# A decoder layer on one core: the convolutions read PSUM, four banks held throughout, and the last two chunks' down rows in one sum

## The chip, the cores and the metric

The kernel runs on one core of one Trainium2 chip. The core has five engines, each with its own queue of instructions, worked off in order: TensorE (PE in the profile, with its weight loads as PEld) does the matmuls and writes only to PSUM; VectorE (DVE) and ScalarE (ACT) do elementwise work and read and write both SBUF and PSUM; GpSimd (POOL) does elementwise work on SBUF; SyncE (SP) issues most DMAs. PSUM has eight banks of 128 partitions x 512 float32. The metric is the device time of one execution in microseconds (us).

## The reference

One decoder layer for 1024 tokens of width 1024, all in float32. The first half of the layer is a token mixer: two groups of heads (chunked gated linear attention, and sliding-window attention with sinks), an output projection and a residual. The change is almost wholly in the second half, the gated MLP:

```
x = x + concat([o_gla, o_swa]) @ w_out
h2 = rms_norm(x, ffn_norm)
u = causal_dwconv(h2 @ w_up, conv_w, conv_b)        # 3 taps along the tokens, per channel, plus a bias
a, b = split(u, 2)                                   # 2816 channels each
out = x + (silu(a) * b) @ w_down
```

The convolution takes, for each channel and token t, `u[t]*w2 + u[t-1]*w1 + u[t-2]*w0 + bias`, with zeros ahead of the first token.

## The kernel before

**Numbers.** Each float32 operand of a large matmul is split into a high part and a low part (`split`, L82: ACT casts the high part, VectorE or GpSimd subtracts it to get the low part), and a product is three passes of matmuls, high x high, high x low, low x high (`PASSES`). A matmul here has 128 x 128 weights and 512 columns.

**Chunks.** The 2816 channels are 22 chunks of 128. For chunk `ch` the up projection gives an a side (`ua`, to be gated by SiLU) and a b side (`ub`), each 128 channels x 1024 tokens, that is two halves of 512 tokens per side. The two sides and the two token halves together are a 2 x 2 block product with the inner dimension cut in two, and chunks 1 to 20 compute it with seven products instead of eight (a Strassen-Winograd form): `SEQ` = P1, P2, P6, P5, P7, P3, P4, each of 12 matmuls. P6, P7 and P4 are added onto the bank of P1, P3 onto the bank of P5 (`ONTO`, L734), so a chunk has three banks. What a bank holds after each product is one of the four results, or a part of it:

- after P1, copied to SBUF by ACT (`ca`, first half); P2 + that copy = a side, first half
- after P6, copied to SBUF (`ca`, second half); after P5, copied to SBUF (`p5`); P7's bank + `p5` = b side, second half
- P3's bank + `ca`, second half = a side, second half
- after P4, the bank of P1 itself is the b side, first half

Chunks 0 and 21 (`PLAIN`) use the eight ordinary products in four banks: P1, R1, P2, R2, X1 to X4.

**After each product** `post` (L782) does the elementwise work: VectorE adds the copy to the bank, with the sum in SBUF (`ca`, `p5`); ACT forms `u = y*w2 + bias` and VectorE adds two taps (`conv` L759, `tap` L756), each one `scalar_tensor_tensor` over 512 tokens (511 or 510 where it starts a half). Where a half continues the one before it, `conv_edge` (L767) adds the first two columns from the last two columns of the half before. ACT takes SiLU of the a side, and VectorE multiplies a and b (`glu`, L778). The sums of the a side lie side by side in `ca`, so its second half needs no edge.

**The down projection** also runs in pairs of chunks, with seven products of two units each (`down_pair`, L894): a unit is six matmuls into a pair of banks, then one VectorE add of 1024 columns onto the accumulator `acc` in SBUF (L908). The operand sums of a pair are made on VectorE (`down_g`, L881: L885 to L889) and GpSimd (`down_w`). `dg` and `dw` are the split operands. The ten pairs are chunks 0 to 19. Chunks 20 and 21 go row by row: `down_row(ch, t)` (L925) does one chunk's contribution to 128 tokens, six matmuls into a pair of banks, then one add of 1024 columns for chunk 20, or two adds of 512 and two stores to DRAM for chunk 21. Five rows of chunk 20 are placed among the products of chunk 21 (`LAST_ROWS`).

**Banks.** `bank()` takes tiles by turns from one pool of eight banks. Just ahead of chunk 2 `open_banks` (L610) closes this pool and opens two others in its place: `psu`, four single banks taken by turns for P1, P2 and P5, and `psd`, two pairs for the down projection. A tile waits until what its memory held before has been read.

**The order.** A list of events with due times (`at`, `at_us`) sets the order in which the code issues work: one product (`MM` = 2.8) and one unit (`UNIT` = 1.4) by turns from chunk 2 on, two units per product near the end. A scheduler with a model of the engines' times may still exchange instructions on an engine's queue.

## Time and profile before

| | |
|---|---|
| median of 3 runs | 1130.04 us (1128.08 to 1131.04) |
| the profiled execution | 1130.23 us |
| its span, first to last instruction | 1128.5 us |
| TensorE matmuls | 1080.7 us busy (96%), 5156 |
| VectorE | 865.9 us (77%), 1251 |
| GpSimd | 689.9 us (61%), 518 |
| ScalarE | 478.0 us (42%), 946 |
| HBM traffic | 55 GB/s over the span |

The busy share in 40 equal slices of 28.2 us, in tenths (9 is 90% or more), with the granted TensorE clock in tenths of full speed:

```profile
PE   7999999999999999699999999999999999999897
DVE  6647456766231588668989999999989898999967
POOL 5456323334450456767878798887878787978420
PEclk9999999999999999899999999999999999999999
```

The mixer and the output projection fill the first 15 slices. The seventeenth, where TensorE falls to 0.6, holds chunks 0 and 1 of the MLP; then VectorE is at 0.8 or above until the end. A row of the timeline reads: start in us, duration, engine, line, instruction, output <- inputs, shapes, count, and in brackets the idle time ahead of it with what ended it. Matmuls are pipelined: one shows about 0.4 us, though the next starts sooner.

### The profile page before, as it was taken

The numbers are of one execution on the slowest core, as the hardware profiler recorded it, in microseconds if no ns is written. First come the engines' busy times: TensorE is split into PE (matmuls) and PEld (weight loads), VectorE is DVE, ScalarE is ACT, GpSimd is POOL, SyncE is SP. The second block draws the span as 40 slices with busy tenths as digits, with TensorE's granted clock in tenths as the row PEclk, the third lists the DMA queues.
The fourth block names the chain that finished last, engine by engine and source line by source line (L and its number), as shares of the span: only waits on it lengthen the run. The fifth ranks groups of instructions, "written<-read, shape, count | busy, mean of one in ns | idle before, by whom it ended". The sixth has DMA issues, their size and how long they took to land.

```text
span 1128.5 us, 14126 instructions
## 1 busy us (share of the span) xinstructions
PE 1080.7 (96%) x5156; PEld 860.6 (76%) x5156; DVE 865.9 (77%) x1251; ACT 478.0 (42%) x946; POOL 689.9 (61%) x518
## 2 busy tenths in 40 slices
PE   7999999999999999699999999999999999999897
PEld 5897777777888878588787777878787878777684
DVE  6647456766231588668989999999989898999967
ACT  5326664434230354434444444344443444443430
POOL 5456323334450456767878798887878787978420
PEclk9999999999999999899999999999999999999999
DMA  6124123002034201112111111112121211111103
GB/s 209 46 77 122 41 57 75 20 1 76 1 108 153 57 1 56 56 38 75 38 56 37 50 45 57 56 47 66 38 75 38 75 37 46 36 51 55 57 1 149
DMA packets 67344, 67.16 MB, mean 60 GB/s; under 512 B 4616, under 2 KB 51913, under 8 KB 67274
## 3 DMA queue, kind: packets, MB, share of 16 engines
q1 hardware_dynamic: 63432, 61.53, 17.4%
q10 hardware_dynamic: 3842, 4.73, 1.8%
q8 instruction: 41, 0.67, 0.3%
q14 instruction: 29, 0.24, 0.1%
HBM read 57.33 MB, written 4.19 MB: 55 GB/s over the span
## 4 chain that ended last, share of the span: by engine, by line
PE 67%; DVE 27%; issue 2%; ACT 2%; DMA 1%; POOL 0%; SPq 0%; ACTq 0%; POOLq 0%
PE P L749 20%; PE dn_P L904 11%; PE do L286 5%; DVE ub L757 4%; DVE ua L757 4%; PE dg L286 4%; PE dr L286 4%; DVE acc L908 4%; PE dv L286 4%; PE dq L286 3%; DVE ub L780 3%; DVE dg L87 2%; PE X L749 2%; PE dk L286 2%; DVE ub L887 1%
## 5 line engine op out<-in xcount | busy, mean ns | idle before, releaser
L904 PE MATMUL dn_P<-dw,dg 128*128 128x512 f32 x840 | 217.8, 394 | 21.3 <-DVE acc L908 14.4
L904 PEld LDWEIGHTS dn_P<-dw,dg 128*128 128x128 f32 x840 | 155.7, 188 | 65.3 <-DVE acc L908 19.9
L908 DVE TENSOR_TENSOR acc<-acc,dn_P 128x1024 f32<-128x1024 f32 x140 | 169.5, 1211 | 41.2 <-PE dn_P L904 41.0
L757 DVE SCALAR_TENSOR_TENSOR ua<-ca,cc,ua 128x511 f32<-128x511 f32 (+1 forms) x80 | 95.9, 1199 | 2.7 <-ACT ua L762 1.8
L87 POOL TENSOR_TENSOR dw<-dn,dw 128x512 fp32r<-128x512 f32 x50 | 82.9, 1658 | 19.4 <-ACT dw L84 19.4
L286 PE MATMUL do<-wow,big 128*128 128x512 f32 x384 | 91.6, 397 | 0.0
L286 PEld LDWEIGHTS do<-wow,big 128*128 128x128 f32 x384 | 71.5, 188 | 16.9 <-ACT wow L84 0.2
L749 PE MATMUL P<-big,A11w 128*128 128x512 f32 x264 | 68.0, 406 | 10.4 <-DVE ub L757 9.5
L424 POOL TENSOR_TENSOR pr<-pr,sm 128x1024 f32<-128x1024 f32 (+1 forms) x16 | 28.6, 1788 | 66.9 <-DVE sm L422 51.2
L749 PEld LDWEIGHTS P<-big,A11w 128*128 128x128 f32 x264 | 50.8, 194 | 23.7 <-issue 9.9
L749 PE MATMUL P<-big,A12w 128*128 128x512 f32 x264 | 65.5, 396 | 0.0
L780 DVE TENSOR_TENSOR ub<-ua,ub 128x512 f32<-128x512 f32 (+1 forms) x45 | 63.1, 1402 | 0.8
L757 DVE SCALAR_TENSOR_TENSOR ub<-p,cc,ub 128x511 f32<-128x511 f32 (+1 forms) x40 | 57.2, 1431 | 4.5 <-ACT ub L762 4.1
L749 PE MATMUL P<-ex,S3w 128*128 128x512 f32 x240 | 59.6, 397 | 0.2 <-ACT ca L793 0.2
L749 PE MATMUL P<-big,S1w 128*128 128x512 f32 x240 | 59.7, 396 | 0.0
L749 PE MATMUL P<-ex,S2w 128*128 128x512 f32 x240 | 59.7, 396 | 0.0
L749 PE MATMUL P<-ex,A22w 128*128 128x512 f32 x240 | 59.7, 396 | 0.0
L749 PE MATMUL P<-big,S4w 128*128 128x512 f32 x240 | 59.6, 396 | 0.0
L762 ACT ACTIVATE ua<-ca,cc 128x512 f32<-128x512 f32 x40 | 32.7, 818 | 62.9 <-DVE ca L804 44.2
L749 PEld LDWEIGHTS P<-big,A12w 128*128 128x128 f32 x264 | 49.6, 188 | 11.8 <-ACT early L821 0.2
L87 DVE TENSOR_TENSOR dg<-ub,dg 128x512 fp32r<-128x512 f32 x40 | 54.3, 1357 | 2.4 <-ACT dg L84 0.5
L749 PEld LDWEIGHTS P<-ex,S3w 128*128 128x128 f32 x240 | 45.0, 188 | 11.4 <-ACT ca L793 0.6
(424 smaller groups left out, 2499.5 us busy)
## 6 DMA issues: line engine op xcount, KB each, us to landing
up<-in_w_up_dram SPq DMA_DIRECT2D x44, 512.0 KB, 3.8
dn<-in_w_down_dram SPq DMA_DIRECT2D x22, 512.0 KB, 3.5
acc<-in_x_dram SPq DMA_DIRECT2D x8, 512.0 KB, 7.7
out_dram<-acc SPq DMA_DIRECT2D x16, 256.0 KB, 2.1
xt<-in_x_dram SPq DMA_DIRECT2D x7, 512.0 KB, 4.3
qraw<-in_w_in_dram SPq DMA_DIRECT2D x4, 512.0 KB, 8.1
vraw<-in_w_in_dram SPq DMA_DIRECT2D x4, 512.0 KB, 3.5
qt<-qt ACTq DMA_DIRECT2D x16, 128.0 KB, 2.3
```

Source lines behind the costliest of these rows:

```text
L87: (eng or pool).tensor_sub(lo, src, hi.bitcast(F32))
L286: pe.matmul(pb[:, :n], lhsT=big[:, t, k, ra, :], rhs=ws[k][:, rb, :n], start=(k == 0 and i == 0), stop=(k == KD - 1 and i == 2))
L424: pool.tensor_tensor(pr[:, :, s0:], pr[:, :, s0:], den[:, hs].rearrange("p (j o) -> p j o", o=1).broadcast_to((P, 4, n)), ALU.mult)
L749: pe.matmul(pb[:, ts.start * P:ts.stop * P], lhsT=w[:, ra, k, :], rhs=b_operand(bn, k, rb)[:, ts], start=(onto is None and i == 0), stop=( ...
L757: dve.scalar_tensor_tensor(dst, src, w, dst, op0=ALU.mult, op1=ALU.add)
L762: act.activation(u[:, a:z], y[:, a:z], AF.Identity, bias=b, scale=w2)
L780: dve.tensor_mul(ub, psb["ua", ch][:, hf * 512 + a:hf * 512 + z], ub)
L887: dve.tensor_sub(a21, a11, a21)
L904: pe.matmul(pb[:, i], lhsT=g[:, ra, c:c + P], rhs=w[:, rb, :], start=(onto is None and n == 0), stop=(n == 2), skip_group_check=onto is no ...
L908: dve.tensor_add(acc, acc, pb)
```

## The change

- `bank()` takes tiles by turns from two pools of four banks, `psa` and `psb`. `open_banks` now runs ahead of chunk 1 instead of chunk 2. It closes only `psb`, puts the two pairs of the down projection there, and takes the four banks of `psa` as fixed tiles `fb0` to `fb3` that stay until the end.
- From chunk 1 on, P1, P2 and P5 of a chunk go to three of these in rotation (`up_bank`), so that the next chunk's P1 gets this chunk's P2 bank, its P2 this chunk's P5 bank, and its P5 this chunk's P1 bank. The fourth holds the b side's second half.
- The sums stay in PSUM: the adds of P2 and P3 write back into the bank, the add of P7 writes into the fourth bank, and the taps read them there. For the b side the last tap writes its sum back into the bank (`conv_in_bank`), and the gate product reads that bank (`glu_from_bank`); its first two columns, which come from the edge, are multiplied apart.
- The a side's halves now lie in two banks, so its second half needs an edge: ACT copies the last two columns of the first half to a small tile `e`, and two taps of one and two columns add them.
- P5's copy goes to `ca`; the tile `p5` is gone.
- `down_row` is replaced by `last_row(t)`: for each half of the columns, six matmuls of chunk 20 and chunk 21 are summed in one bank, then one add of 512 columns and one store. Rows 0, 1, 4, 5 use the pairs, rows 2, 3, 6, 7 the fixed banks. All eight rows come after the last product.

```diff
     ps_first = ExitStack()
-    ps = {"b": ps_first.enter_context(tc.tile_pool(name="ps", bufs=8, space=PSUM))}
+    ps = {"a": ctx.enter_context(tc.tile_pool(name="psa", bufs=4, space=PSUM)),
+          "b": ps_first.enter_context(tc.tile_pool(name="psb", bufs=4, space=PSUM)), "n": 0}
 
     def bank(name):
-        return ps["b"].tile([P, 512], F32, tag="b", name=name)
+        ps["n"] += 1
+        return ps["ab"[ps["n"] % 2]].tile([P, 512], F32, tag="b", name=name)
...
     def open_banks():
         ps_first.close()
-        ps["b"] = ctx.enter_context(tc.tile_pool(name="psu", bufs=4, space=PSUM))
         ps["d"] = ctx.enter_context(tc.tile_pool(name="psd", bufs=2, space=PSUM))
+        ps["f"] = [ps["a"].tile([P, 512], F32, tag="b", name=f"fb{i}") for i in range(4)]
...
+    ORDER = {"P1": 0, "P2": 1, "P5": 2}
+    ORDER_PLAIN = {"P1": 0, "R1": 1, "X1": 2, "X3": 3}
+
+    def up_bank(ch, name):
+        i = (ORDER_PLAIN if ch in PLAIN else ORDER)[name]
+        return ps["f"][3 if i == 3 else (ch - 1 + i) % 3]
...
+    def conv_in_bank(ch, u, y):
+
+        ci = NCH + ch
+        w0, w1, w2, b = (cc[:, i, ci:ci + 1] for i in range(4))
+        act.activation(u, y, AF.Identity, bias=b, scale=w2)
+        tap(u[:, 1:512], y[:, 0:511], w1)
+        dve.scalar_tensor_tensor(y[:, 0:510], y[:, 0:510], w0, u[:, 2:512], op0=ALU.mult, op1=ALU.add)
+
+    def glu_from_bank(ch, hf, y):
+        u = psb["c", ch, hf]
+        ua = psb["ua", ch][:, hf * 512:hf * 512 + 512]
+        dve.tensor_mul(u[:, 2:512], ua[:, 2:512], y[:, 0:510])
+        dve.tensor_mul(u[:, 0:2], ua[:, 0:2], u[:, 0:2])
...
         elif name == "P2":
-            ca = psb["ca", ch]
-            dve.tensor_add(ca[:, 0:512], ca[:, 0:512], pb)
+            dve.tensor_add(pb, psb["ca", ch][:, 0:512], pb)
             ua = psb["ua", ch] = wide_tile(f"ua{ch}", "ua")
-            conv(ch, 0, ua, ca, 0, 512, True)
+            conv(ch, 0, ua, pb, 0, 512, True)
+            e = psb["e", ch] = fin["ff"].tile([P, 2], F32, tag="e", name=f"e{ch}", bufs=2)
+            act.copy(e, pb[:, 510:512])
...
         elif name == "P5":
-            p5 = psb["p5", ch] = half_tile(f"p5_{ch}")
-            act.copy(p5, pb)
+            act.copy(psb["ca", ch][:, 0:512], pb)
         elif name == "P7":
-            p5 = psb["p5", ch]
-            dve.tensor_add(p5, p5, pb)
+            v = psb["v", ch] = ps["f"][3]
+            dve.tensor_add(v, psb["ca", ch][:, 0:512], pb)
             ub = psb["c", ch, 1] = half_tile(f"ub1_{ch}")
-            conv(ch, 1, ub, p5, 0, 512, True)
+            conv_in_bank(ch, ub, v)
         elif name == "P3":
-            ca, ua = psb["ca", ch], psb["ua", ch]
-            dve.tensor_add(ca[:, 512:], ca[:, 512:], pb)
-            conv(ch, 0, ua, ca, 512, 1024, False)
+            ua = psb["ua", ch]
+            dve.tensor_add(pb, psb["ca", ch][:, 512:], pb)
+            conv(ch, 0, ua[:, 512:], pb, 0, 512, True)
+            conv_edge(ch, 0, ua[:, 512:], psb["e", ch])
             silu(ua)
         elif name == "P4":
             ub = psb["c", ch, 0] = half_tile(f"ub0_{ch}")
-            conv(ch, 1, ub, pb, 0, 512, True)
+            conv_in_bank(ch, ub, pb)
             conv_edge(ch, 1, psb["c", ch, 1], pb[:, 510:512])
-            glu(ch, 0)
-            glu(ch, 1)
+            glu_from_bank(ch, 0, pb)
+            glu_from_bank(ch, 1, psb["v", ch])
...
+    def last_row(t):
+        if t % 4 < 2:
+            pair = two_banks(f"dl{t}")
+            pbs = [pair[:, 0], pair[:, 1]]
+        else:
+            pbs = [ps["f"][i] for i in ((2, 0), (1, 3))[t % 4 - 2]]
+        for hf, pb in enumerate(pbs):
+            for ch in (NCH - 2, NCH - 1):
+                g, w = gtiles[ch, t // 4], blocks["d", ch, hf]
+                for i, (ra, rb) in enumerate(PASSES[::-1]):
+                    pe.matmul(pb, lhsT=g[:, ra, (t % 4) * P:(t % 4 + 1) * P], rhs=w[:, rb, :],
+                              start=(ch == NCH - 2 and i == 0), stop=(ch == NCH - 1 and i == 2))
+            acc, cs = fin["all"][:, t], slice(hf * 512, hf * 512 + 512)
+            dve.tensor_add(acc[:, cs], acc[:, cs], pb)
+            sp.dma_start(out[t * P:(t + 1) * P, cs], acc[:, cs])
...
-    at_us(starts[2, 0] - 0.05, open_banks)
+    at_us(starts[1, 0] - 0.05, open_banks)
```

What this does to the queues is shown at three places. First TensorE, from P3 of chunk 1 to P6 of chunk 2 (A11w, A12w and so on are the split weights of the products: A11w is P1's, A12w P2's, S2w P6's, S1w P5's, S3w P7's, S4w P3's, A22w P4's; P_1 and P_2 are tiles of chunks 1 and 2). Before:

```order
L749 MATMUL P_1_4451<-big,S4w_4465 128x512 x12
L749 MATMUL P_1_4390<-ex,A22w_4484 128x512 x12
L749 MATMUL P_2_4552<-big,A11w_4514 128x512 x12
L749 MATMUL P_2_4589<-big,A12w_4534 128x512 x12
L904 MATMUL dn_P_0_4610<-dw_0_4491,dg_0_4494 128x512 x6
L904 MATMUL dn_P_1_4634<-dw_0_4491,dg_0_4494 128x512 x4
L749 MATMUL P_2_4552<-ex,S2w_4569 128x512 x12
```

And now (the fixed banks are fb):

```order
L759 MATMUL fb_4399<-big,S4w_4475 128x512 x12
L759 MATMUL fb_4398<-big,A11w_4523 128x512 x11
L759 MATMUL fb_4397<-ex,A22w_4493 128x512 x12
L759 MATMUL fb_4398<-big,A11w_4523 128x512
L929 MATMUL dn_P_0_4616<-dw_0_4500,dg_0_4503 128x512 x6
L929 MATMUL dn_P_1_4640<-dw_0_4500,dg_0_4503 128x512 x6
L759 MATMUL fb_4399<-big,A12w_4545 128x512 x12
L759 MATMUL fb_4398<-ex,S2w_4574 128x512 x12
```

P1 of chunk 2 has moved ahead of P4 of chunk 1, since it no longer shares a pool with it, and the first unit of the down projection ahead of P2.

Second VectorE, from the end of chunk 9 to the sums for the fifth pair of the down projection (ub is the b side, ua the a side, D the pair's sums). Before:

```order
L757 SCALAR_TENSOR_TENSOR ub_9_6332<-P_9_6122,cc,ub_9_6332 128x510
L757 SCALAR_TENSOR_TENSOR ub_9_6271<-P_9_6122,cc,ub_9_6271 128x1
L780 TENSOR_TENSOR ub_9_6332<-ua_6174,ub_9_6332 128x512
L757 SCALAR_TENSOR_TENSOR ub_9_6271<-P_9_6122,cc,ub_9_6271 128x2
L780 TENSOR_TENSOR ub_9_6271<-ua_6174,ub_9_6271 128x512
L885 TENSOR_TENSOR D_4_6401<-ub_8_6047,ub_9_6271 128x512
L908 TENSOR_TENSOR acc<-acc,dn_P_1_6370 128x2x512
L886 TENSOR_TENSOR D_4_6402<-D_4_6401,ub_8_6107 128x512
```

And now:

```order
L798 SCALAR_TENSOR_TENSOR fb_4399<-fb_4399,cc,ub_9_6352 128x510
L804 TENSOR_TENSOR ub_9_6352<-ua_6192,ub_9_6352 128x2
L803 TENSOR_TENSOR ub_9_6289<-ua_6192,fb_4400 128x510
L767 SCALAR_TENSOR_TENSOR ub_9_6289<-fb_4399,cc,ub_9_6289 128x1
L767 SCALAR_TENSOR_TENSOR ub_9_6289<-fb_4399,cc,ub_9_6289 128x2
L803 TENSOR_TENSOR ub_9_6352<-ua_6192,fb_4399 128x510
L804 TENSOR_TENSOR ub_9_6289<-ua_6192,ub_9_6289 128x2
L933 TENSOR_TENSOR acc<-acc,dn_P_1_6391 128x2x512
L910 TENSOR_TENSOR D_4_6421<-ub_8_6063,ub_9_6289 128x512
L911 TENSOR_TENSOR D_4_6422<-D_4_6421,ub_8_6125 128x512
```

Each gate product has become one with an operand in a bank and one of two columns, and the unit's add stands ahead of the pair's sums instead of between them.

Third TensorE behind the last product (dn_0, dl_9121 and so on are banks of the rows, dnw_0 and dnw_1 the two halves of the down weights, g the gated product; of two tiles of one name the higher number is chunk 21's). Before, from X4 on:

```order
L749 MATMUL X_21_9079<-big,A22w_8948 128x512 x12
L933 MATMUL dn_2_9016<-dnw_0_8911,g_0_8914 128x512 x3
L933 MATMUL dn_2_9016<-dnw_1_8951,g_0_8914 128x512 x3
L933 MATMUL dn_3_9024<-dnw_0_8911,g_0_8914 128x512 x3
L933 MATMUL dn_3_9024<-dnw_1_8951,g_0_8914 128x512 x3
L933 MATMUL dn_4_9032<-dnw_0_8911,g_1_8954 128x512 x3
```

And now:

```order
L759 MATMUL fb_4400<-big,A22w_8990 128x512 x12
L960 MATMUL dl_9121<-dnw_0_8954,g_0_8957 128x512 x3
L960 MATMUL dl_9138<-dnw_0_8954,g_0_8957 128x512 x3
L960 MATMUL fb_4399<-dnw_0_8954,g_0_8957 128x512
L960 MATMUL dl_9121<-dnw_0_9013,g_0_9069 128x512 x3
L960 MATMUL dl_9138<-dnw_0_9013,g_0_9069 128x512 x3
L960 MATMUL fb_4399<-dnw_0_8954,g_0_8957 128x512 x2
L960 MATMUL fb_4399<-dnw_0_9013,g_0_9069 128x512 x3
```

Before, six rows of chunk 20 and then eight of chunk 21 follow X4, each with its own banks; now each bank takes three matmuls of chunk 20 and three of chunk 21, over the pairs and the fixed banks.

More of the change, by code (lines that the diff above doesn't have):

```diff
@@ L741, in product @@
         if onto is None and not part:
-            psb[name, ch] = bank(f"{name}_{ch}")
+            psb[name, ch] = up_bank(ch, name) if ch else bank(f"{name}_{ch}")
         pb = psb[name, ch] = psb[onto or name, ch]
@@ L923, in g_split @@
         split(ub[:, a:z], g[:, 0, a:z], g[:, 1, a:z], dve)
-    def down_row(ch, t):
-        pb = two_banks(f"dn{ch}_{t}")
-        g = gtiles[ch, t // 4]
-        acc = fin["all"][:, t]
-        last = ch == NCH - 1
-        for hf in range(2):
-            w = blocks["d", ch, hf]
-            for i, (ra, rb) in enumerate(PASSES[::-1] if last else PASSES):
-                pe.matmul(pb[:, hf], lhsT=g[:, ra, (t % 4) * P:(t % 4 + 1) * P], rhs=w[:, rb, :],
-                          start=(i == 0), stop=(i == 2))
-            if last:
-                cs = slice(hf * 512, hf * 512 + 512)
-                dve.tensor_add(acc[:, cs], acc[:, cs], pb[:, hf])
-                sp.dma_start(out[t * P:(t + 1) * P, cs], acc[:, cs])
-        if not last:
-            dve.tensor_add(acc, acc, pb.rearrange("p h n -> p (h n)"))
+    def last_row(t):
[13 more added lines that the diff above has]
+            sp.dma_start(out[t * P:(t + 1) * P, cs], acc[:, cs])
     ev = []
@@ L1046, in hymba_layer_kernel @@
     units = [(p, k, j) for p in range(NPAIR) for k in range(7) for j in range(2)]
-    rows = [(NCH - 2, t) for t in range(NT)]
-    LAST_ROWS = {2: 2, 3: 3}
     prods, starts, unit_at, tu = [], {}, {}, 0.0
@@ L1071, in hymba_layer_kernel @@
                     tu += UNIT
-            if ch == NCH - 1:
-                for _ in range(LAST_ROWS.get(i, 0)):
-                    at_us(tu, down_row, *rows.pop(0))
-                    tu += UNIT
     for i, name in enumerate(("P1", "R1", "P2", "R2")):
@@ L1124, in hymba_layer_kernel @@
     at_us(starts[L, 5] + MM - 0.2, lambda: g_open(L, 1, U_SLOT[L, "A12"]))
-    for ch, t in rows + [(L, t) for t in range(NT)]:
-        at_us(tu, down_row, ch, t)
-        tu += UNIT
+    for t in range(NT):
+        at_us(tu, last_row, t)
+        tu += MM
     for _, _, f, a in sorted(ev, key=lambda e: e[:2]):
```

## The prediction

> **What bounds the kernel now.** I read first the table of busy time by stage (columns: stretch, its length, busy time and instructions of PE, PEld, DVE, ACT, POOL, then granted clock, DMA share, GB/s). I cut it at the first product of chunk 3, the first product of chunk 21, the end of the last product, and the last matmul.
>
> ```profile
> 509.05:1064.72 555.67, 534.39 (x2276) 425.40 (x2274) 518.32 (x499) 242.38 (x398) 448.62 (x295) 1.00 0.17 52
> 1064.72:1099.55 34.83, 34.83 (x152) 28.18 (x151) 25.68 (x31) 13.79 (x24) 10.28 (x8) 1.00 0.05 16
> 1099.55:1124.60 25.05, 22.91 (x85) 14.10 (x83) 21.17 (x34) 1.91 (x4) 0.00 (x0) 1.00 0.36 137
> ```
>
> Chunks 3 to 20 take half the span. TensorE is busy 96% of it, but VectorE is nearly full too: 518.3 of 555.7 us, or 28.8 us for each of the 18 chunks. What TensorE takes when nothing holds it up is in two rows of the timeline (start, duration, instruction):
>
> ```profile
> 709.80 2.98 PE L749 MATMUL P<-ex,S3w 128*128 128x512 f32 x12
> 714.00 2.98 PE L749 MATMUL P<-big,S4w 128*128 128x512 f32 x12
> ```
>
> Between them lie one product and one unit of the down projection, 18 matmuls in 4.20 us, 0.233 us each. The 2274 weight loads of the stage stand for as many matmuls: 2274 x 0.233 = 530 us. So **about 25.7 us of that stage are waits of TensorE**. The table of waits says for whom (total, times, longest):
>
> ```profile
> PE dn_P L904 <- DVE acc L908: 14.4, 10, 2.0
> PE P L749 <- DVE ub L757: 9.5, 1, 9.5
> PE dn_P L904 <- ACT dw L84: 5.7, 8, 0.8
> PE dn L933 <- DVE acc L940: 1.4, 4, 0.6
> ```
>
> Rows one and three return once per pair of chunks; they are 20.1 us plus some 0.2 us of pipeline refill each. One instance:
>
> ```profile
> 737.34 1.21 DVE L908 TENSOR_TENSOR acc<-acc,dn_P 128x1024 f32<-128x1024 f32 x1
> 738.47 1.61 DVE L889 TENSOR_TENSOR D<-ub,D 128x512 f32<-128x512 f32 x1
> 740.00 3.47 DVE L757 SCALAR_TENSOR_TENSOR ua<-ca,cc,ua 128x511 f32<-128x511 f32 x2
> 743.39 1.21 DVE L908 TENSOR_TENSOR acc<-acc,dn_P 128x1024 f32<-128x1024 f32 x1
> 744.65 1.64 PE L904 MATMUL dn_P<-dw,dg 128*128 128x512 f32 x6 [1.53 <-DVE acc L908]
> ```
>
> The unit needs its pair of banks emptied by the add at 743.39, and that add stands behind two convolution taps that took 3.47 us. VectorE falls behind where the pair's extra sums (L885 to L889) are made, and TensorE waits there. So the bound is TensorE with a VectorE that is late in bursts. Two single places come on top: one wait of 9.5 us before chunk 2, and the rows at the end.
>
> **The change, part by part. 1: the convolutions on VectorE.** Groups of instructions, 520 to 1050 us (last columns: count, busy, mean ns, idle before):
>
> ```profile
> L780 DVE TENSOR_TENSOR ub<-ua,ub 128x512 f32<-128x512 f32 x34 | 51.1, 1504 | 0.6
> L757 DVE SCALAR_TENSOR_TENSOR ua<-ca,cc,ua 128x512 f32<-128x512 f32 x34 | 35.1, 1032 | 0.3
> L757 DVE SCALAR_TENSOR_TENSOR ub<-p,cc,ub 128x510 f32<-128x510 f32 x17 | 29.5, 1734 | 0.3
> L757 DVE SCALAR_TENSOR_TENSOR ua<-ca,cc,ua 128x511 f32<-128x511 f32 x17 | 25.6, 1505 | 0.0
> L757 DVE SCALAR_TENSOR_TENSOR ua<-ca,cc,ua 128x510 f32<-128x510 f32 x18 | 24.0, 1334 | 0.3
> L757 DVE SCALAR_TENSOR_TENSOR ub<-p,cc,ub 128x511 f32<-128x511 f32 x17 | 21.1, 1238 | 0.0
> L757 DVE SCALAR_TENSOR_TENSOR ub<-P,cc,ub 128x511 f32<-128x511 f32 x17 | 12.6, 741 | 0.0
> L757 DVE SCALAR_TENSOR_TENSOR ub<-P,cc,ub 128x510 f32<-128x510 f32 x17 | 12.6, 740 | 0.0
> L799 DVE TENSOR_TENSOR p<-p,P 128x512 f32<-128x512 f32 x17 | 11.5, 676 | 0.9 <-PE P L749 0.9
> L757 DVE SCALAR_TENSOR_TENSOR ub<-P,cc,ub 128x2 f32<-128x2 f32 x17 | 3.5, 208 | 0.0
> ```
>
> The same tap takes 740 ns with P (PSUM) as its source and 1030 to 1730 ns with ca or p (SBUF). Before, per chunk: three adds 3 x 0.676, taps of P2 1.505 + 1.334, of P7 1.238 + 1.734, of P3 2 x 1.032, of P4 0.741 + 0.740, two edge taps 0.42, two gate products 2 x 1.504: 14.8 us. After, all eight full taps read PSUM, 8 x 0.74, the adds stay, the gate products read one operand from PSUM (I take the add's 0.676), two edge taps 0.42: 5.92 + 2.03 + 1.35 + 0.42 = 9.72 us. New are four tiny operations with both tensors in SBUF: the two edge taps of P3 (from e) and the two-column gate products. Such operations stand only in the plain chunks now:
>
> ```profile
> 450.71 1.73 POOL L87 TENSOR_TENSOR S2w<-up,S2w 128x512 fp32r<-128x512 f32 x1
> 451.22 1.24 DVE L757 SCALAR_TENSOR_TENSOR ua<-e,cc,ua 128x1 f32<-128x1 f32 x1
> 454.29 0.21 DVE L757 SCALAR_TENSOR_TENSOR ua<-e,cc,ua 128x2 f32<-128x2 f32 x1
> 454.42 0.74 DVE L757 SCALAR_TENSOR_TENSOR ub<-early,cc,ub 128x511 f32<-128x511 f32 x1
> ```
>
> One column took 1.24 us while POOL was in an instruction, two columns 0.21 us while POOL was idle (the last row is a full tap from SBUF with POOL idle: 0.74, as from PSUM). Bounds for the four: 0.84 to 5.0 us. POOL is busy 81% of the stage, with instructions of about 1.5 us, so the mean wait is some 0.81 x 0.75 = 0.6 us and the four cost 3.3 us. Post-processing then goes from 14.8 to 13.0 us per chunk (10.6 to 14.7), VectorE from 28.8 to 27.0 us, against TensorE's 29.4. By the mean of the idle and the busy row alone it would be 2.9 us for the four, nearly the same. The Trainium skill, SBUF — State Buffer, "Who interferes with whom", says that a VectorE instruction with two SBUF inputs waits out a whole GpSimd instruction that reads SBUF, whatever its size; taken with POOL always busy that is the 5.0 us end, post-processing at 14.7 and no relief, and the 0.21 row is why I don't take it.
>
> No row shows VectorE writing PSUM, and five full operations per chunk now do, four of them in the bank they read. Bounds: as SBUF writes (0 us), or reading and writing one bank by turns, twice as long (four times 0.7, 2.8 us per chunk); below nothing isn't excluded, but no row has such an operation under 0.67. I take 0, as reading PSUM costs nothing visible beside SBUF (0.74 in both).
>
> More than the mean matters the burst. In the instance above the two taps shrink from 3.47 to 1.48, and the two gate products and taps ahead of the pair's sums lose another 2 us or so; the wait is 1.5 to 2 us. So it should close in most pairs. Late next is ACT: the new copy of e waits until VectorE's taps have read the bank, and behind it in ACT's queue stand the casts of dw and dg and the copy of P5, for which P3 waits. The second tap, at 743.5 in the instance, would end some 4 us sooner, near 739.5, the copy of P5 three or four ACT instructions later, near 742; P3 is due near 744.5 (the unit above without its wait, 743.1, and its 1.4): some 2 us of slack. I leave a fifth of the waits: **20.5 of 25.7 us gained** (bounds 0 and 25.7).
>
> **2: the entry into chunk 2.** Now the pools change there, and the first product waits until the old eight banks are all read:
>
> ```profile
> 466.61 2.96 PE L749 MATMUL P<-ex,A22w 128*128 128x512 f32 x12
> 479.10 3.32 PE L749 MATMUL P<-big,A11w 128*128 128x512 f32 x7 [9.53 <-DVE ub L757]
> 470.00:479.00 9.00, 0.00 (x0) 0.00 (x0) 8.01 (x10) 3.04 (x4) 9.00 (x7) 0.68 0.00 0
> 479.10:483.90 4.80, 4.80 (x12) 3.81 (x13) 4.59 (x5) 0.62 (x1) 2.47 (x2) 0.55 0.00 0
> 465.18 1.30 POOL L87 TENSOR_TENSOR A11w<-up,A11w 128x512 fp32r<-128x512 f32 x1
> 469.09 1.71 POOL L87 TENSOR_TENSOR A12w<-up,A12w 128x512 fp32r<-128x512 f32 x1
> 478.23 1.72 POOL L87 TENSOR_TENSOR dw<-T,dw 128x512 fp32r<-128x512 f32 x1
> 485.37 1.28 POOL L87 TENSOR_TENSOR S1w<-S,S1w 128x512 fp32r<-128x512 f32 x1 [3.71 <-ACT S1w L84]
> 499.27 1.55 PE L904 MATMUL dn_P<-dw,dg 128*128 128x512 f32 x6
> ```
>
> After, the pools change ahead of chunk 1, and P1 of chunk 2 goes to a bank that is free. A11w is ready at 466.5, so P1 runs from about 466.6, P4 of chunk 1 until 472, both halves of unit 0 until 474.8, P2 (A12w ready at 470.8) until 477.6, P6 until 480.4. What is late next is POOL: S1w comes after dw at 479.95, so at about 481.7, which holds P5 by 0.8 us; S3w comes three POOL instructions of 1.3 to 1.75 us later, at 486.5, which holds P7 by about 2 us more. P7 and unit 1 end near 491.8; before, that point is 499.27 + 1.4 = 500.7. **Gain 9 us** (bounds 0, if another wait takes its place, and 11.5, the 9.5 and 2.0 of slow clock). The 2.0 is in it: the 12 matmuls after the gap took 4.8 us at a clock of 0.55, against 12 x 0.233 = 2.8. The Trainium skill, TensorE: Matmul & The Clock Gate, "HAM oscillation — how this bites in real kernels", puts the limit for idle gaps at about 3.4 us; the trace agrees so far that 9 us lowered the clock and the waits of up to 2.0 us in chunks 3 to 20 left it at 1.00. By that rule a P7 held for 3.4 us would cost another 2 us, and the gain would be 7.
>
> **3: the rows of the last two chunks.** Now chunk 20 has eight rows with adds of 1024 columns and chunk 21 eight rows with two adds of 512 each, through two pairs of banks:
>
> ```profile
> 1099.55 2.90 PE L933 MATMUL dn<-dnw,g 128*128 128x512 f32 x12
> 1120.76 0.53 PEld L933 LDWEIGHTS dn<-dnw,g 128*128 128x128 f32 x3 [0.17 <-DVE acc L937]
> 1121.07 1.38 DVE L937 TENSOR_TENSOR acc<-acc,dn 128x512 f32<-128x512 f32 x2 [0.36 <-PE dn L933]
> ```
>
> Behind the last product 84 matmuls remain, 19.6 us of work in 25.05 us. After, 96 remain (12 no longer sit inside the products, which end 2.8 us sooner), with 16 adds of 0.69 us instead of eight of 1.2 and 16 of 0.69, over eight banks. VectorE then has 11 us of adds and about 5 us of chunk 21's post-processing beside 22.4 us of matmuls, so it doesn't hold them up. 25.05 - 19.6 = 5.4, less 0.2 of drain and a little for the first rows: **gain 5 us** (bounds 0 and 5.4). The last add and the store behind it stay.
>
> The front's banks still alternate over eight; a few transposes and small matmuls change places: 0, bounds 2 us either way.
>
> **Sum.** The profiled execution took 1130.23 us (span 1128.5), 0.2 us above the median. 1130.2 - 20.5 - 9 - 5 = 1095.7.
>
> **Rivals.** (a) The bursts stay: the copy of e holds ACT, dw or P5's copy come late, and only some 9 us of the 25.7 go: 1130.2 - 9 - 9 - 5 = 1107. For it: only about 2 us of slack once per pair; against it: only that place is so tight. (b) The entry to chunk 2 finds another wait of the same length (the rows of w_down, or POOL's queue): 1130.2 - 20.5 - 5 = 1104.7. Against it: at 470 POOL already has A11w, A12w and the first dw. (c) Slower: VectorE becomes the bound, because an operation in its own bank takes double and the tiny ones take 1.24 us each. Post-processing is then 9.72 + 2.8 + 5.0 = 17.5, VectorE 31.5 us per chunk; at the 93% it reaches now that is 33.8 us per chunk against 30.9, 52 us more in all, less the 14 of parts 2 and 3: 1168. It decides from about 0.8 us per chunk above today's 14.8. Against it: it takes both upper ends at once. (d) No change: TensorE's waits come from something that the edits don't touch; the wait rows speak against it.
>
> **How the numbers follow.** My forecast (1088 to 1101) 0.66, (a) 0.19, (b) 0.08, (c) 0.04, (d) 0.03. The low end is all three bounds together, 1130.2 - 25.7 - 11.5 - 5.4 = 1087.6; the high end, 1111, takes in (b) and (a) with some ends worse. Within 0.3% is about what a measurement of this kernel can't tell from no change. Faster 0.93, same 0.03, slower 0.04.
>
> **What would show it.** Full taps and gate products near 0.74 and 0.68 us with PSUM sources; tiny gate products with a mean well above 0.21; the waits on L908's line under 5 us in total; no gap over 3.4 us near 470 and a clock of 1.00 there; 96 matmuls in about 22.5 us at the end. Wrong it would be if an add into PSUM took 1.3 us, if VectorE stayed above 93% busy, or if TensorE waited for ACT's casts in each pair.

## The result, and the profile after

The changed kernel takes 1094.71 us (median of four runs, 1093.49 to 1101.03), beside 1130.54 for the kernel before on the same chip. The ratio is 0.970 (95% interval 0.966 to 0.974). Forecast were 1095.7 us, with a range of 1087.6 to 1111. The profiled execution took 1095.48 us, with a span of 1093.8. Three experiments below had one execution each that was far longer than their others (`x_dve2` 1172 us at a granted clock of 0.85, `x_act3` 1510 at 0.66, `a_cast` 2145); the times given leave these out, and no waits are read from the trace of `x_dve2`, which is of that execution.

The busy time by stage, cut at the same four points as before (first product of chunk 3, of chunk 21, end of the last product, last matmul):

```profile
504.37:1035.56 531.19, 531.19 (x2281) 428.53 (x2280) 466.53 (x574) 246.17 (x418) 405.41 (x297) 1.00 0.18 54
1035.56:1067.69 32.13, 32.13 (x139) 25.93 (x138) 22.88 (x31) 13.04 (x23) 10.44 (x8) 1.00 0.06 17
1067.69:1089.94 22.25, 22.25 (x97) 17.83 (x95) 13.81 (x27) 1.91 (x4) 0.00 (x0) 1.00 0.44 166
```

TensorE is busy for the whole of all three stretches; nothing holds it up from chunk 3 to the last matmul. VectorE has 466.5 / 18 = 25.9 us per chunk where it had 28.8. In the table of waits, TensorE no longer waits for acc at all; these are its four longest (total, times, longest):

```profile
PE mix L980 <- DMA mix_row<-in_mix_norm_dram: 3.0, 1, 3.0
PE P L759 <- ACT early L846: 2.4, 1, 2.4
PE n1pt L246 <- DVE n11v L168: 1.9, 1, 1.9
PE kpt L356 <- DVE kn L347: 1.3, 1, 1.3
```

All of them stand in the front. VectorE's groups, 500 to 1020 us, show what the new operations cost (last columns: count, busy, mean ns, idle before):

```profile
L767 DVE SCALAR_TENSOR_TENSOR ua<-fb,cc,ua 128x511 f32<-128x511 f32 x36 | 26.7, 741 | 0.8 <-ACT ua L772 0.8
L798 DVE SCALAR_TENSOR_TENSOR fb<-fb,cc,ub 128x510 f32<-128x510 f32 x35 | 26.2, 749 | 0.3
L803 DVE TENSOR_TENSOR ub<-ua,fb 128x510 f32<-128x510 f32 x36 | 24.3, 675 | 0.0
L804 DVE TENSOR_TENSOR ub<-ua,ub 128x2 f32<-128x2 f32 x36 | 21.5, 598 | 0.0
L812 DVE TENSOR_TENSOR fb<-ca,fb 128x512 f32<-128x512 f32 x18 | 12.4, 689 | 2.5 <-PE fb L759 2.5
L767 DVE SCALAR_TENSOR_TENSOR ua<-e,cc,ua 128x1 f32<-128x1 f32 x18 | 9.3, 516 | 0.0
L767 DVE SCALAR_TENSOR_TENSOR ua<-e,cc,ua 128x2 f32<-128x2 f32 x18 | 7.7, 426 | 0.0
```

The tap that writes the bank it reads takes 0.749 us, the sum written to PSUM 0.689: a PSUM output costs about 0.01 us here (0.74 and 0.676 with outputs in SBUF). The two-column gate product takes nearly as long in the mean (0.598) as the one of 510 columns (0.675).

The parts, measured between marks that both traces have. The first product of chunk 1, and the end of unit 1 of chunk 2:

```profile
457.06 2.97 PE L759 MATMUL fb<-big,A11w 128*128 128x512 f32 x12
494.62 2.92 PE L929 MATMUL dn_P<-dw,dg 128*128 128x512 f32 x12
497.37 2.97 PE L759 MATMUL fb<-big,S4w 128*128 128x512 f32 x12
```

and of the kernel before, the same two marks:

```profile
449.31 2.97 PE L749 MATMUL P<-big,A11w 128*128 128x512 f32 x12
500.66 2.97 PE L749 MATMUL P<-big,S4w 128*128 128x512 f32 x12
```

| stretch | before, us | after, us | gain | forecast |
|---|---|---|---|---|
| front, to the first product of chunk 1 | 449.3 | 457.1 | -7.8 | 0 (2 either way) |
| entry, to the end of unit 1 | 51.4 | 40.3 | 11.0 | 9 |
| chunks 2 to 21, to the end of the last product; the 12 moved matmuls (2.8) counted here in both | 598.9 | 573.1 | 25.8 | 20.5 |
| last rows, without those 12 | 28.9 | 23.3 | 5.6 | 5 |
| span | 1128.5 | 1093.8 | 34.7 | 34.5 |

That the sum came out within 1 us is luck, since two misses cancel: the front is 7.8 us slower, outside its bounds, and the other three parts together gave 8 us more than forecast.

### The profile page after: what moved, and what is told of

Same layout as the page of the kernel before. It is cut to its first block, busy times and chain, and to the rows that moved or that the text cites. A ratio compares the mean times of both kernels' runs of the same rounds, so it can differ in the third digit from the quotient of the medians.

```text
span 1093.8 us, 14260 instructions
## 1 busy us (share of the span) xinstructions
PE 1079.5 (99%) x5156; PEld 867.3 (79%) x5156; DVE 797.0 (73%) x1323; ACT 480.6 (44%) x966; POOL 641.5 (59%) x518
## 4 chain that ended last, share of the span: by engine, by line
PE 93%; DVE 4%; DMA 1%; ACT 1%; issue 0%; POOL 0%; SPq 0%; ACTq 0%; POOLq 0%
PE fb L759 36%; PE dn_P L929 17%; PE do L288 7%; PE dg L288 4%; PE dr L288 4%; PE dv L288 4%; PE dq L288 3%; PE dk L288 2%; PE pv L449 1%; PE ppt L437 1%; PE dq L646 1%; PE X L759 1%; PE fb L960 1%; PE dl L960 1%; PE go L552 1%; PE go L548 1%
## 5 line engine op out<-in xcount | busy, mean ns | idle before, releaser
L759 PE MATMUL fb<-big,A11w 128*128 128x512 f32 x264 | 66.4, 396 | 0.0
L759 PE MATMUL fb<-big,A12w 128*128 128x512 f32 x264 | 65.6, 396 | 0.0
L767 DVE SCALAR_TENSOR_TENSOR ua<-fb,cc,ua 128x511 f32<-128x511 f32 x82 | 60.7, 741 | 4.2 <-ACT ua L772 3.7
L759 PE MATMUL fb<-big,S1w 128*128 128x512 f32 x240 | 60.0, 397 | 0.3 <-DVE ub L803 0.3
L759 PE MATMUL fb<-ex,S3w 128*128 128x512 f32 x240 | 59.7, 397 | 0.2 <-ACT ca L818 0.2
L759 PE MATMUL fb<-big,S4w 128*128 128x512 f32 x240 | 59.8, 396 | 0.0
L759 PE MATMUL fb<-ex,S2w 128*128 128x512 f32 x240 | 59.6, 396 | 0.0
L759 PE MATMUL fb<-ex,A22w 128*128 128x512 f32 x240 | 59.5, 397 | 0.0
L759 PEld LDWEIGHTS fb<-big,A11w 128*128 128x128 f32 x264 | 49.6, 188 | 12.0
L759 PEld LDWEIGHTS fb<-big,A12w 128*128 128x128 f32 x264 | 49.7, 188 | 11.7
```

The lines of the kernel that those rows point to most:

```text
L759: pe.matmul(pb[:, ts.start * P:ts.stop * P], lhsT=w[:, ra, k, :], rhs=b_operand(bn, k, rb)[:, ts], start=(onto is None and i == 0), stop=( ...
L767: dve.scalar_tensor_tensor(dst, src, w, dst, op0=ALU.mult, op1=ALU.add)
```

## The experiments

The kernel before ran beside each group of experiments; ratios are to that.

**Does the order in the front cost the time?** In `b_pools` the kernel before gets only the two pools by turns:

```diff
-    ps = {"b": ps_first.enter_context(tc.tile_pool(name="ps", bufs=8, space=PSUM))}
+    ps = {"a": ps_first.enter_context(tc.tile_pool(name="psa", bufs=4, space=PSUM)),
+          "b": ps_first.enter_context(tc.tile_pool(name="psb", bufs=4, space=PSUM)), "n": 0}
...
-        return ps["b"].tile([P, 512], F32, tag="b", name=name)
+        ps["n"] += 1
+        return ps["ab"[ps["n"] % 2]].tile([P, 512], F32, tag="b", name=name)
...
-        ps["b"] = ctx.enter_context(tc.tile_pool(name="psu", bufs=4, space=PSUM))
+        ps["a"] = ps["b"] = ctx.enter_context(tc.tile_pool(name="psu", bufs=4, space=PSUM))
```

> The kernel before, with one edit: the front takes its banks by turns from two pools of four, as the change does, in place of one pool of eight; everything from chunk 1 on is as before. The order of the instructions up to chunk 0 is then that of the changed kernel, row for row. Theory A (the order costs the time that the front lost): P1 of chunk 1 starts 6 to 8 us later than the 449.3 of before, near 457, and the time is 1136 to 1139 us. Theory B (the front's time varies from one execution to the next, and the order has no price): P1 of chunk 1 starts at 449 to 451, and the time is 1129 to 1132.

Measured: 1136.09 us, ratio 1.0055 (1.0042 to 1.0068), so 5 to 8 us slower. The changed kernel again, beside it:

> The changed kernel once more, to see what its front does in another execution. Theory A (order): P1 of chunk 1 starts at 455 to 458 again, and the time is 1093 to 1096. Theory B (variation): P1 of chunk 1 starts anywhere from 449 to 457, and the executions spread over some 8 us.

Measured: 1097.27 us (1094.9 to 1099.44), 0.971 (0.969 to 0.972); the first product of chunk 1 starts at 456.70, and in `b_pools` at 453.83. Theory A holds, the order has a price, but its number for `b_pools` was too high: 4.5 us later than before, not 6 to 8. The profiled execution of `b_pools` reaches the stage below 1.7 us sooner than that of the changed kernel, and has no slow clock (1.5 us) in chunk 0. Two places pay the price. The first is the stage from the first matmul of the gate projection (dg) to the first of the next one (dr). Columns: stretch, length, busy time of PE, PEld, DVE, ACT, POOL, clock, DMA share, GB/s; before, then after:

```profile
170.09:270.79 100.70, 99.14 (x688) 78.74 (x685) 71.14 (x216) 43.70 (x127) 34.33 (x27) 1.00 0.15 39
```

```profile
170.76:276.13 105.37, 104.72 (x687) 81.58 (x686) 71.30 (x216) 43.55 (x130) 34.18 (x27) 1.00 0.14 37
```

The same matmuls, 5.6 us more of busy TensorE. The length is 105.34 in `b_pools` and 105.36 in the second execution, so it doesn't vary. Grouped by line, the masked scores (ga) stand out; before, then after:

```profile
L535 PE MATMUL ga<-gqt 64*128 64x128 f32 x56 | 5.1, 297 | 0.0
```

```profile
L537 PE MATMUL ga<-gqt 64*128 64x128 f32 x56 | 8.5, 297 | 0.7 <-DVE ql L393 0.7
```

Their rows in the timeline tell why; token tiles 1 and 6 of the changed kernel:

```profile
205.50 0.71 PE L537 MATMUL ga<-gqt 64*128 64x128 f32 x4
212.61 0.71 PE L537 MATMUL ga<-gqt 64*128 64x128 f32 x4
...
275.48 0.72 PE L537 MATMUL ga<-gqt 64*128 64x128 f32 x8
```

One group of four works in rows 0 to 63 of the array, the other in rows 64 to 127. Where the groups stand together, eight take 0.72 us; where other matmuls part them, four take as long. Before, all eight pairs stand together; in the changed kernel five are parted, which is 5 x 0.7 = 3.5 us.

The second place is chunk 0. ScalarE's copy of its first bank, before, then after:

```profile
430.68 0.59 ACT L821 COPY early<-P 128x512 f32<-128x512 f32 x1 [1.24 <-PE P L749]
```

```profile
436.40 0.62 ACT L86 CAST ex<-t 128x512 fp32r<-128x512 f32 x1 [3.72 <-DVE t L236]
436.93 0.58 ACT L846 COPY early<-P 128x512 f32<-128x512 f32 x1
```

Now it stands behind a cast that waits 3.72 us for VectorE, and P2, whose tiles wait for the copy, starts 2.41 us late:

```profile
437.56 4.61 PE L759 MATMUL P<-big,A12w 128*128 128x512 f32 x12 [2.41 <-ACT early L846]
```

Its 12 matmuls then took 4.61 us at a lowered clock, against 2.99 before.

**The order of before, with the rest of the change.** In `f_close` the front has one pool of eight, closed ahead of chunk 1; in `f_one` nothing is closed. The diff is that of `f_one`, shortened; its units also add 512 columns at a time:

```diff
...
     def open_banks():
-        ps_first.close()
-        ps["d"] = ctx.enter_context(tc.tile_pool(name="psd", bufs=2, space=PSUM))
-        ps["f"] = [ps["a"].tile([P, 512], F32, tag="b", name=f"fb{i}") for i in range(4)]
+        ps["f"] = [bank(f"fb{i}") for i in range(4)]
...
     def two_banks(name):
-        return ps["d"].tile([P, 2, 512], F32, tag="d", name=name)
+        return [bank(f"{name}_{i}") for i in range(2)]
...
```

> The changed kernel, with the front's one pool of eight put back; ahead of chunk 1 it is closed, and the four held banks and the two pairs are opened in its place. The front's order is that of before again. Theory A (order): the front gives back its 7.75 us, and the time is 1087 to 1089, if the first product of chunk 1 finds all eight banks read; if it waits for them as the first product of chunk 2 did before (9.5 us, and 2.0 of slow clock), 1095 to 1099. Theory B (variation): 1094 to 1096 without such a wait, 1103 to 1106 with it.

> The changed kernel with one pool of eight banks for the whole program: the front's order is that of before again, the four held banks are taken from the pool ahead of chunk 1, nothing is closed, and a unit of the down projection takes two single banks with an add of 512 columns each instead of a pair with one add of 1024. Theory A (order of the front): the 7.75 us of the front come back without a wait ahead of chunk 1; VectorE has 2 x 0.69 - 1.21 = 0.17 us more per unit, 0.34 per chunk and a half, hidden: 1087 to 1089. Rival: the second add comes later than the one add did, and TensorE waits for single banks at each unit: 1092 or more, with waits of a unit's matmuls for acc.

`f_close`: 1093.04 us, 0.966 (0.965 to 0.968). The front is that of before again, but the pool change holds the first product of chunk 1, and the clock falls behind it:

```profile
452.85 5.36 PE L758 MATMUL fb<-big,A11w 128*128 128x512 f32 x12 [3.68 <-DVE early L867]
```

That is 3.7 + 2.4 = 6.1 us lost again of the 7.8. The mechanism is that of Theory A's second case, with a shorter wait; the time lies below that case and above the first, in neither range. `f_one`: 1088.69 us, 0.965 (0.963 to 0.968), with no such wait:

```profile
449.12 2.97 PE L753 MATMUL fb<-big,A11w 128*128 128x512 f32 x12
```

This version is faster than both kernels; its span is 1087.0. Of the 7.9 us that its front is shorter than the changed kernel's, 1.1 are lost again in the entry (to the same mark, 41.4 us instead of 40.3), where a unit waits 0.92 us for a cast of ScalarE. Its runs fall in two groups, three at 1087.9 to 1088.7 and two at 1094.7; what the two lost in wasn't seen, since the profiled execution was one of the fast three.

**The parted pairs alone.** `s_split0` is `f_one` with the pairs parted on purpose:

```diff
-        at(s + 1.9, gla_a, t)
+        at(s + 1.9, gla_a, t, (0,))
+        at(s + 2.0, gla_a, t, (1,))
```

> The version with one pool of eight banks for the whole program (f_one), with one edit in the front: the two pairs of matmuls of the masked scores (ga, on the lower and on the upper 64 rows of the array) are issued as two events, so that a row of the gate projection (dg, 24 matmuls) stands between them, for all eight token tiles; almost nothing else changes place. In the changed kernel's front five of the eight pairs were parted by other matmuls. Mine (two pairs that stand together run side by side in 0.72 us, two that are parted take 0.71 us each): the stage from the first dg to the first dr goes from 100.70 us to about 105.6 (seven pairs x 0.7), and the time is 5 to 6 us above that of f_one, 1093 to 1095. Rival (the stage's 4.7 us came from other instructions that changed places): the stage stays within 1 us of 100.7, and the time at 1088 to 1090.

Measured: 1094.71 us, 0.970 (0.968 to 0.972), 6.0 us above `f_one` (5.3 by the ratios). The stage:

```profile
169.25:274.01 104.76, 104.07 (x684) 81.32 (x682) 72.70 (x219) 44.42 (x129) 35.68 (x28) 1.00 0.15 41
```

4.06 us more than the 100.70 of before. Up to the first dr 13 groups of four stand alone, 13 x 0.71 = 9.2, where before seven pairs took 7 x 0.72 = 5.0: 4.2 expected on that count, a little under the seven full pairs of the expectation. For all eight pairs it would be 8 x 0.70 = 5.6 us, and the first product of chunk 1 starts 5.5 us later than in `f_one`:

```profile
454.60 2.97 PE L753 MATMUL fb<-big,A11w 128*128 128x512 f32 x12
```

The price of parting is shown.

**The copy alone.** `a_cast` moves the cast ahead of the copy to VectorE, for token tile 6:

```diff
-        put(t4, ex[:, 2, i], dve)
+        split(t4, ex[:, 2, i, :, 0, :], ex[:, 2, i, :, 1, :], dve, dve if t == 6 else None)
```

> The changed kernel with one cast of the front (the high part of T4 for token tile 6) moved from ScalarE to VectorE, where its source is made. Then the copy of chunk 0's first bank no longer stands behind it in ScalarE's queue. Theory A (one wait of the new order, 2.42 us, with the slow clock behind it where that comes, 1.55 us more): both go, P1 of chunk 1 starts 2 to 4 us sooner, at 453 to 455, and the time is 2 to 4 us under the changed kernel's. Rival: the wait is only passed on, to the transposes and X products behind it, which wait for VectorE: within 1 us of the changed kernel.

Measured: 1094.41 us, 0.968 (0.966 to 0.971), in two groups, 1090.8 and 1091.8, then 1097.0 and 1098.0; this isn't told apart from the changed kernel (0.971, 0.969 to 0.972, in `a_again`). The profiled execution is the slowest of the four, and its trace says where its gain went. The first product of chunk 1 starts at 453.53, 3.5 us sooner, as Theory A had it; but then P5 of chunk 2 waits for its bank, which chunk 1's gate product still reads:

```profile
489.00 5.44 PE L759 MATMUL fb<-big,S1w 128*128 128x512 f32 x12 [4.02 <-DVE ub L803]
```

In the changed kernel that wait is 0.34 us. The gate product (488.17) is late because a two-column product ahead of it in VectorE's queue, 0.20 us in the changed kernel, lasted through three instructions of GpSimd in a row:

```profile
482.83 3.91 DVE L804 TENSOR_TENSOR ub<-ua,ub 128x2 f32<-128x2 f32 x1
488.17 0.68 DVE L803 TENSOR_TENSOR ub<-ua,fb 128x510 f32<-128x510 f32 x1
482.97 1.30 POOL L901 TENSOR_TENSOR T<-dn,T 128x512 f32<-128x512 f32 x1
484.22 1.28 POOL L89 TENSOR_TENSOR dw<-dn,dw 128x512 fp32r<-128x512 f32 x1
485.46 1.26 POOL L89 TENSOR_TENSOR S3w<-up,S3w 128x512 fp32r<-128x512 f32 x1
```

So this is not a wait that comes with every earlier front: in `f_one`, whose front is 8 us shorter than the changed kernel's, P5 of chunk 2 doesn't wait. Neither theory had it. Whether the two faster executions went without it isn't shown, as neither was traced.

**What took the 25.8 us away?** `a_sbuf` has the elementwise work of before in the changed kernel's banks (P2's part of the edit; the other products' parts go back in the same way):

```diff
         elif name == "P2":
-            dve.tensor_add(pb, psb["ca", ch][:, 0:512], pb)
+            ca = psb["ca", ch]
+            dve.tensor_add(ca[:, 0:512], ca[:, 0:512], pb)
...
-            conv(ch, 0, ua, pb, 0, 512, True)
+            conv(ch, 0, ua, ca, 0, 512, True)
```

> The changed kernel with the elementwise work after each product of chunks 1 to 20 as before: sums, taps and gate products in SBUF. Pools, held banks, front and last rows stay as changed. Mine (the bursts of VectorE came from operands in SBUF, and PSUM as their source took them away): the 25.8 us between chunk 2 and the last product go again, the waits for acc at each pair come back, and the time is 1118 to 1122. Rival (the held banks took TensorE's waits away, whatever VectorE reads): 1095 to 1100, with no waits for acc.

Measured: 1122.56 us, 0.993 (0.991 to 0.995). That is 0.6 us above the range expected. The waits of before (14.4 and 5.7) are back:

```profile
PE dn_P L928 <- DVE acc L932: 14.3, 10, 2.0
PE dn_P L928 <- ACT dw L86: 4.4, 8, 0.8
```

So it is where VectorE's operands lie, not the held banks. In `a_glu` only the b side's last tap and the gate products go back to SBUF:

```diff
-            conv_in_bank(ch, ub, v)
+            conv(ch, 1, ub, v, 0, 512, True)
...
-            conv_in_bank(ch, ub, pb)
+            conv(ch, 1, ub, pb, 0, 512, True)
...
-            glu_from_bank(ch, 0, pb)
-            glu_from_bank(ch, 1, psb["v", ch])
+            glu(ch, 0)
+            glu(ch, 1)
```

> The changed kernel, with all sums in PSUM and all taps reading it, but the b side's last tap and both gate products with SBUF operands, as before; the two-column gate products go with that. By the rows, VectorE has 2 x (1.504 - 0.675) - 2 x 0.598 = 0.46 us more per chunk. Mine: VectorE, 73% busy, has that to spare, no burst comes back, and the time stays within 1 us of the changed kernel's in the same session, near 1095 to 1097. Rival: long gate products beside GpSimd just ahead of a pair's sums are what made the bursts; waits for acc return in most pairs, 0.5 to 1 us each, and the time is 1100 to 1106.

Measured: 1096.32 us, 0.971 (0.969 to 0.972), the ratio of the changed kernel. Between 500 and 1020 us TensorE is busy throughout, and VectorE has 453.4 us, less than the 455.9 of the changed kernel in the same stretch. The gate products take longer, but the two tiny ones of each chunk are saved:

```profile
L790 DVE TENSOR_TENSOR ub<-ua,ub 128x512 f32<-128x512 f32 x36 | 48.0, 1333 | 0.6
```

2 x 1.333 = 2.67 us per chunk, against 2 x (0.675 + 0.598) = 2.55. So the gate products from PSUM bring nothing here; with `a_sbuf`, what is left for the gain are the sums and the other taps.

**How much is there to spare?** `x_dve2` and `x_dve5` add copies of P3's bank onto itself behind its taps, two or five per chunk; `x_act3` adds three such copies on ScalarE behind the copy of e:

```diff
             conv_edge(ch, 0, ua[:, 512:], psb["e", ch])
+            for _ in range(5):
+                dve.tensor_copy(pb, pb)
```

> The changed kernel with VectorE loaded on purpose: after the taps of P3, just ahead of where a pair's sums are made, it copies the bank onto itself twice per chunk (nothing else changes, and the values stay). At about 0.65 us each that is 1.3 us more per chunk: VectorE goes from 458.5 of 522.6 us, 25.8 per chunk of 29.4, to 27.1. Mine (the bursts are gone with a margin): TensorE's waits for acc stay under 3 us in all, 1095 to 1100. Rival (the bursts are only just covered): a wait of 0.5 us or more comes back in most pairs, 5 to 10 us in all, 1101 to 1107.

> The same with five such copies per chunk, 3.2 us: VectorE is at 29.0 us per chunk, the 28.8 that it had before the change, against TensorE's 29.4. Mine (what counts is VectorE's load in the burst, whatever instructions make it up): the waits for acc are back at about the 14 to 26 us of before, 1110 to 1123. Rival (the long waits came from the operands in SBUF themselves, beside GpSimd, and not from VectorE's load): under 6 us of waits, below 1102.

> The changed kernel with ScalarE loaded on purpose: behind the copy of e, in the bank of P2, it copies the bank onto itself three times per chunk, 3 x 0.59 = 1.8 us ahead of the casts of the next operands and of P5's copy, for which P3 waits. Mine (some 2 us of slack there, as the prediction worked out): P3 waits at most a few tenths in some chunks, under 3 us in all, 1095 to 1099. Rival (a) of the prediction (ScalarE is the next to be late): P3 or a unit waits for ScalarE 0.5 us and more in most chunks, 1103 to 1115.

`x_dve2` took 1094.38 us, 0.969 (0.966 to 0.971): no cost by its times. `x_dve5` took 1122.43, 0.993 (0.989 to 0.996), `x_act3` 1096.58, 0.969 (0.967 to 0.972). From 500 to 1020 us, the kernel before, then `x_dve5` and its longest wait:

```profile
500.00:1020.00 520.00, 502.14 (x2140) 400.20 (x2139) 484.35 (x466) 228.94 (x375) 423.57 (x279) 1.00 0.17 52
```

```profile
500.00:1020.00 520.00, 502.36 (x2141) 401.27 (x2140) 469.28 (x622) 229.77 (x391) 382.61 (x279) 1.00 0.17 52
```

```profile
PE dn_P L931 <- DVE acc L935: 17.5, 9, 2.1
```

A copy takes 0.688 us by its group's mean, so the work after the products goes from 11.9 us per chunk (worked out below) to 15.3, near the 14.8 of before; and TensorE is idle for 520 - 502.4 = 17.6 us, as it was for 17.9 before, though every full tap still takes 0.74 us from PSUM. So what the work is made of doesn't count for these waits. Nor does the mean load alone: VectorE is busy for 469 us here and for 484 before, with the same waits. Somewhere between 2 x 0.688 = 1.4 and 5 x 0.688 = 3.4 us more per chunk the spare time at that place ends. In `x_act3`, with 1.8 us more on ScalarE:

```profile
500.00:1020.00 520.00, 520.00 (x2233) 419.52 (x2233) 456.74 (x562) 267.51 (x458) 404.54 (x294) 1.00 0.18 53
```

TensorE doesn't wait in this stretch; the slack ahead of P5's copy is at least that. Before it, in chunk 1, the extra work does show once: P7 waits 2.06 us for ScalarE's copy of P6, where it waits 0.21 in the changed kernel:

```profile
467.88 3.08 PE L759 MATMUL fb<-ex,S3w 128*128 128x512 f32 x12 [2.06 <-ACT ca L820]
```

**The last rows.** `a_rows` has the rows of before:

```diff
-    for t in range(NT):
-        at_us(tu, last_row, t)
-        tu += MM
+    for ch, t in rows + [(L, t) for t in range(NT)]:
+        at_us(tu, down_row, ch, t)
+        tu += UNIT
```

> The changed kernel, with the rows of the last two chunks as before: eight rows of chunk 20, five of them among the products of chunk 21, then eight of chunk 21, all through the two pairs of banks. Mine: the shared sum and the eight banks are worth 5.6 us there, so 1099 to 1101, with about 5 us of TensorE's waits and of its refill behind the last product. Rival: the rows at the end were held by VectorE's backlog from chunk 21, which the convolutions shrink anyway, so the edit of the rows brings under 2 us: 1095 to 1096.5.

Measured: 1099.43 us, 0.973 (0.971 to 0.975). The waits are back behind the last product:

```profile
1068.75 2.90 PE L958 MATMUL dn<-dnw,g 128*128 128x512 f32 x12
1071.93 1.63 PE L958 MATMUL dn<-dnw,g 128*128 128x512 f32 x6 [0.28 <-DVE acc L965]
...
1080.54 13.19 PE L958 MATMUL dn<-dnw,g 128*128 128x512 f32 x45 [0.54 <-DVE acc L965]
```

From there to the end of the span (1097.6) are 28.85 us, as before; the changed kernel takes 26.1 from its last product with 12 matmuls (2.8 us) more in them. That is 5.6 us in the trace, though the medians, 1097.27 for the changed kernel run beside it and 1099.43, differ by only 2.2 and the intervals of the two ratios overlap, so the price is read from the traces: this execution's front was 1.5 us shorter than the changed kernel's. VectorE's smaller load doesn't mend these rows; the rival falls.

## Why the prediction was right

**The bound and the main mechanism: right.** TensorE was held by VectorE's bursts where a pair's sums are made, and operands in PSUM took the bursts away (`a_sbuf`). The size was off: "I leave a fifth of the waits" failed, none are left. The fifth stood for ScalarE coming late, with 2 us of slack; `x_act3` shows that from 500 us on 1.8 us of extra work there cost nothing, and the times of `x_dve2` that VectorE has 1.4 to spare as well.

**VectorE's cost per chunk: 13.0 us forecast, 11.9 measured** from the groups' means. The full taps (0.74) and writes into the bank (0, of bounds 0 to 2.8) came as said. The four tiny operations take 2 x 0.598 + 0.516 + 0.426 = 2.14 us, not 3.3: the mean wait behind GpSimd is shorter than 0.81 x 0.75 us, and GpSimd itself is less busy, 405 of 531 us instead of 449 of 556. Taken singly, though, the 1.24 us that the prediction took as the upper bound of one isn't a bound: one took 2.56 us in `f_close` and one 3.91 in `a_cast`. Edge taps whose source is PSUM stay at 0.21. The Trainium skill, SBUF — State Buffer, "Who interferes with whom", has such operations wait for GpSimd, which the prediction priced at 5.0 us for the four with GpSimd always busy; these rows agree that they wait, and put the four at 2.14.

**The entry: right in kind.** 11.0 instead of 9, because P5 and P7 of chunk 2, for which 2.8 us of waits for GpSimd were forecast, waited only 0.34 together, and that for VectorE. This isn't secure: the same P5 waited 0.49 us in `a_rows`, 1.43 in `f_close`, 2.62 in `a_glu` and 4.02 in `a_cast`, each time for VectorE. (The slice of the page before in which TensorE falls to 0.6 is this place: 451 to 479 us, chunk 1 and the wait of 9.5 us behind it; chunk 0 lies ahead of it.)

**The last rows: right,** 5.6 instead of 5 (`a_rows`).

**The front: wrong.** "A few transposes and small matmuls change places: 0, bounds 2 us either way" is the step that failed. Eight banks taken by turns from two pools are not the eight banks of one pool: each tile must wait for a bank of its own four, and the order follows that. It cost 4.7 us in the gated attention, of which the parted pairs are 3.5 (`s_split0` shows the price) and 1.2 are spread over other small groups and not followed further; then 2.4 for the copy behind a cast, and in this execution 1.6 of slow clock. Of these 8.7 us some 0.9 came back elsewhere in the front.

**The rivals.** (a) fell: from chunk 2 on the changed kernel's TensorE doesn't wait for ScalarE, nor does it under the load of `x_act3`. (b) didn't occur in the changed kernel, where the entry gained 11.0; the waits of P5 just named are of its kind, for VectorE instead. (c) fell with its two prices: the bank that is read and written costs nothing extra, and a tiny operation 0.43 to 0.60 us in the mean, not 1.24. `x_dve5` shows that more work on VectorE does bring its waits back, at 15.3 us per chunk; `x_dve2`, at 13.3, shows no cost. (d) fell with `a_sbuf`.

## What to carry to other kernels

A mean load doesn't say whether an engine is late: move work out of its burst, and measure the spare time by adding work at that place. An edit of buffers that "only" changes which bank a tile takes changes the order of everything that waits for a bank, so read the changed order for pairs that must stand together and for copies that fall in behind a waiting instruction. Look at a stage that gained in more than one execution: an operation of two columns can hold up its queue when it meets several instructions of GpSimd in a row, and so the bank that the next product waits for.

## What the runs showed of the hardware

Matmuls with 64 contraction rows, on the lower and the upper half of the array, run side by side only if they stand next to each other: eight in 0.72 us, four alone in 0.71; parting eight such pairs put off what follows by 5.5 us (`s_split0`). The Trainium skill, TensorEngine Tiling (Array Packing), "Key Properties", says that different tiles can work in parallel; the rows agree, with the condition that nothing stands between them.

An operation of one or two columns with both tensors in SBUF can last through more than one instruction of GpSimd: 2.56 us through two (`f_close`, it ended at 485.90, the second of them at 485.88) and 3.91 us through three (`a_cast`, 486.74 and 486.72), where the mean of such gate products in the changed kernel is 0.60.

Behind the same wait of 2.4 us TensorE's clock was lower in half of the traces that have it. 437 to 442 us in the changed kernel, where the wait ends at 437.56, then in `b_pools`, where it ends at 435.86 (clock: third column from the end):

```profile
437.00:442.00 5.00, 4.44 (x12) 3.50 (x13) 2.02 (x3) 0.99 (x3) 0.06 (x1) 0.66 0.00 0
```

```profile
437.00:442.00 5.00, 5.00 (x31) 4.23 (x30) 2.12 (x4) 1.58 (x3) 0.00 (x0) 1.00 0.02 3
```

Of eight profiled executions with this wait, the 12 matmuls behind it took 4.4 us or more in four and 3.1 in four. What decides between the two isn't shown; it makes 1.5 us of difference between executions of one kernel. The Trainium skill, TensorE: Matmul & The Clock Gate, "HAM oscillation — how this bites in real kernels", puts the limit for such gaps at about 3.4 us; here 2.4 us was followed by the lower clock in half of the cases. Of other waits, 2.06 us (`x_act3`) was followed by 3.1 us for the 12 matmuls, 2.62 (`a_glu`) by 4.6, 3.68 (`f_close`) and 4.02 (`a_cast`) by 5.4, and 4.53 (`x_dve5`) by 4.6.
